# DeltaNet chunk matrices: decays from rows broadcast by DMA instead of a matmul and a transpose

## The chip, the cores and the metric

The kernel runs on one core of one Trainium2 chip. The metric is the device time of one execution in microseconds; the median of several executions is compared. The engines are called PE (TensorE, matmuls), DVE (VectorE), ACT (ScalarE), POOL (GpSimd) and SP (SyncE, which issues most DMAs). Each runs its own queue in order, and waits for the others through semaphores.

## What is computed

One step of a hybrid decoder layer for 256 prompt tokens and for 8 sequences of 4 new tokens (32 sample tokens), in float32. The reference, cut to the part around the change:

```python
h = RMSNorm(x);  q, k, v, z, beta, alpha, ... = split(h @ w_in)       # one projection, 15888 columns
g  = -exp(a_log) * softplus(alpha + dt_bias)                          # decay of a token and head
gc = cumsum(g) within a chunk
diff  = gc[..., :, None] - gc[..., None, :]
decay = where(incl, exp(where(incl, diff, 0)), 0)                     # incl: lower triangle with diagonal
lower = where(strict, (k*beta @ k.T) * decay, 0)                      # strict: without diagonal
tinv  = triangular_solve(eye + lower, eye)
u, w  = tinv @ (v*beta), tinv @ (k*beta*exp(gc))
a_intra = where(incl, (q @ k.T) * decay, 0)
# then a scan over the chunks with the state s0, a gated norm, two more branches
# (dilated attention, pooling), their merge through w_out, and a SwiGLU (w_gu, w_down)
```

There are 8 heads with keys and values of 128. `beta` is sigmoid of its projection, and k and q are scaled to length one.

## The kernel before

All 288 tokens (256 prompt, 32 sample) are the moving side of every dense matmul, 128 x 288; the weights stream in as the stationary side. A weight tile of 512 KB is loaded by SP (`raw`, L169), rounded by ACT to its high part (`wh`, L180), and DVE takes the rest (`wl`, L184). A dense product in float32 is made of three matmuls: wh with the high part of the activations (L256), wh with their low part (L257), wl with the high part (L258). There are some 14,000 of them; they are called dense matmuls here, and are counted to name a place in the program. There are five buffers of `raw` and three each of `wh` and `wl`.

The rest of the layer (the mixer) is written as Python generators, the convolution, `gdn(hg)` for the two head groups hg = 0 and 1 of four heads each, the attention, the pooling. After every weight tile, `step()` advances each of the running generators by its rate (a `yield n` counts n times). So the mixer's instructions come to stand between dense matmuls; a scheduler that plans with a timeline of its own then fixes the order in which each engine's queue stands. At run time nothing is reordered.

`beta_alpha` makes `beta` and the decays `g` for both groups and sums them with triangular ones matrices, `U` (row t, column i, one where t <= i), `V` (t > i) and block versions `Ub` and `Vb` for the sample tokens (blocks of four). It keeps exponentials of the sums (`egc`, `esf`, `egl`) and `g` itself (`gl`). `cp` tiles live through the mixer; `U(...)` takes one of NU slots of 128 x 288.

`gdn(hg)` handles nine matrices of 128 x 128 (x = 0 to 7: four heads times two stretches of 128 prompt tokens; x = 8: the sample tokens of the four heads). Before the change lies the normalisation: `ss` holds 1/|k| and 1/|q| (`rk`, `rq`), `s` = beta/|k|, and `nbe`, `kdc`, `qsc` are scales made from them (L710 to L713). Then, for each x, `gram` holds K K^T and K Q^T (L722); the decay matrix is a matmul of V with U scaled by the decays (`ug`, L720, L723), its exponential (ACT, L726) and a multiplication with U (POOL, L727); `s` is spread along the rows by a transpose of a broadcast column (L724); and DVE multiplies (L730, L732) to `la`, the masked and scaled matrices. `gram` tiles come from a ring of four PSUM buffers. From `la` POOL and DVE pick the diagonal 32 x 32 blocks (`lt`, `ltc`); these go to DRAM (`dlt`, L744) and come back as 32 small systems in 32 partitions (`lb`, L746), which DVE solves in 31 steps of two operations (`tm` L759, `X` L761). Between them, `gdn_sample` does the sample tokens, reading the state by SP (`st`, L891; `st2`, L953): the products `kss` of state and keys (L896), `ys` (L907), `zs` (L911) and `ws` (L915). The copy `ys` (DVE, L912) between `zs` and `ws` stands in DVE's queue among the steps of the solve. The kept matrices x = 0 to 7 go on to the merge of blocks (L775 on), and to the chunk scan.

Of the kernel before, what the change touches and what calls it, by code (L numbers as in the profile page):

```python
# [9 lines left out]
F32 = mybir.dt.float32  # L10
F32R = mybir.dt.float32r
AF = mybir.ActivationFunctionType
OP = mybir.AluOpType
# [6 lines left out]
NU = 98  # L20
# [68 lines left out]
class Layer:  # L89
# [335 lines left out]
    def beta_alpha(self):  # L425
        nc, a, c = self.nc, self.a, self.c
# [4 lines left out]
        p = self.ps("ba")  # L431
        for k in range(4):
            for j in range(4):
                d = j * 4 + k
                nc.tensor.matmul(p[32 * j:32 * j + 32, :NT], lhsT=w[:, d * 16:d * 16 + 32], rhs=self.xT[d],
                                 start=k == 0, stop=k == 3, tile_position=(0, 32 * j))
# [4 lines left out]
        for ch in range(2):  # L441
            nc.tensor.matmul(pt[:, ch * 16:ch * 16 + 16], lhsT=bat[:, ch * 128:(ch + 1) * 128], rhs=c["gsel"],
                             start=True, stop=True)
# [5 lines left out]
        beta = self.cp.tile([128, 2, 9], F32, name="beta")  # L449
# [45 lines left out]
        self.beta, self.gl, self.egc, self.esf, self.egl = beta, g, egc, esf, egl  # L495
# [6 lines left out]
        for hg in range(2):  # L502
            t = ts[hg]
            nc.tensor.matmul(pe[:, hg * 32:hg * 32 + 32], lhsT=c["ones"], rhs=t, start=True, stop=True)
            t2 = self.cp.tile([128, 32], F32, name=f"eglx{hg}")
            nc.scalar.activation(t2, pe[:, hg * 32:hg * 32 + 32], AF.Exp)
            self.egls.append(t2)

# [171 lines left out]
    def gdn(self, hg):  # L680
# [3 lines left out]
        gcol = lambda x: self.gl[:, hg * 9 + x:hg * 9 + x + 1]  # L684
# [29 lines left out]
        yield  # L714
        LA = {}
        ltc = pp.tile([128, 8, 32], F32, name="ltc")
        for x in X9:
            um, vm = (c["Ub"], c["Vb"]) if x == 8 else (c["U"], c["V"])
            ug = self.U(name="ug")
            nc.scalar.activation(ug[:, :128], um, AF.Copy, scale=gcol(x))  # L720
            p = self.ps("gram")
            nc.tensor.matmul(p[:, 0:256], lhsT=kq(x)[:, 0:128], rhs=kq(x)[:, 0:256], start=True, stop=True)  # L722
            nc.tensor.matmul(p[:, 256:384], lhsT=vm, rhs=ug[:, :128], start=True, stop=True)  # L723
            nc.tensor.transpose(p[:, 384:512], s[:, x:x + 1].to_broadcast([128, 128]), c["ident"])  # L724
            dt = ug[:, 128:256]
            nc.scalar.activation(dt, p[:, 256:384], AF.Exp)  # L726
            nc.gpsimd.tensor_tensor(dt, dt, um, op=OP.mult)  # L727
            la = self.U(name="la")
            for q in range(2):
                nc.vector.scalar_tensor_tensor(la[:, q * 128:q * 128 + 128], p[:, q * 128:q * 128 + 128],  # L730
                                               rk[:, x:x + 1], dt, op0=OP.mult, op1=OP.mult)
            nc.vector.tensor_tensor(la[:, 0:128], la[:, 0:128], p[:, 384:512], op=OP.mult)  # L732
            self.free(ug)
# [844 lines left out]
```

## Time and profile before

| | before |
|---|---|
| time, median of 3 runs | 2033.3 us |
| lowest, highest | 2032.03, 2034.34 us |
| the profiled execution | 2031.39 us |
| its span (first to last instruction) | 2029.6 us |
| mean granted clock of PE | 0.997 |

The span is what the views of the trace cover; the execution is 1.8 us longer than it. A row of the views begins with the start (us from the span's start) and the busy time; where instructions are grouped, "x36" counts them and a busy time covers the group. A row's bracket names the idle time before it and what ended it. PEclk and the granted clock are shares of PE's full speed. "SPq" rows are the issuing of DMAs, not their transfer. Matmul rows overlap, since matmuls are pipelined.

### The profile page before, as it was taken

Reading aid. Unit: us, or ns where it says so; the run is one execution under the profiler, and the core shown is the slowest. Engines: PE = TensorE matmul, PEld = TensorE weight load, DVE = VectorE, ACT = ScalarE, POOL = GpSimd, SP = SyncE. Lnnn points to the kernel's source line nnn. Section 1 sums busy time; section 2 is a strip of 40 time slices with the busy share of each in tenths; the row PEclk is TensorE's granted clock in tenths of the full one; section 3 lists DMA queues with packets and bytes.
Section 4 is the critical chain, followed back from the end, with each engine's and each line's share of the span. In section 5 each row is a group of like instructions: output and inputs, shape, how many; then the busy total and the mean of one; then the engine's idle time right before and its main releaser. Section 6 shows DMA issues by size and latency. Waiting matters only on the chain. (4 is left out here: it accounts for less than half of the span.)

```text
span 2029.6 us, 38724 instructions
## 1 busy us (share of the span) xinstructions
PE 2002.6 (99%) x15220; PEld 1979.3 (98%) x15220; DVE 1328.9 (65%) x2855; ACT 896.1 (44%) x1423; POOL 173.0 (9%) x315
## 2 busy tenths in 40 slices
PE   8999999999999999999999999999999999999998
PEld 8999998999999999999999999999999999999998
DVE  7969657658888779998874475544555445554555
ACT  6664464354444344333344454343333333333344
POOL 2325402300000031100000000000000000000001
PEclk9999999999999999999999999999999999999999
DMA  8565646758875567876667656777777677777762
GB/s 272 154 187 167 186 133 184 216 173 278 259 220 170 179 192 218 251 257 210 208 232 232 211 183 218 225 220 226 223 225 222 219 228 220 225 221 228 215 207 91
DMA packets 231350, 425.34 MB, mean 210 GB/s; under 512 B 23344, under 2 KB 67328, under 8 KB 229504
## 3 DMA queue, kind: packets, MB, share of 16 engines
q1 hardware_dynamic: 229856, 420.84, 66.8%
q8 instruction: 119, 1.95, 0.4%
q0 software_dynamic: 1168, 1.45, 0.2%
q10 hardware_dynamic: 144, 0.59, 0.1%
q14 instruction: 63, 0.52, 0.1%
HBM read 410.44 MB, written 66.63 MB: 235 GB/s over the span
## 5 line engine op out<-in xcount | busy, mean ns | idle before, releaser
L184 DVE TENSOR_TENSOR wl<-raw,wh 128x1024 fp32r<-128x1024 f32 x585 | 719.5, 1231 | 515.4 <-ACT wh L180 509.9
L180 ACT CAST wh<-raw 128x1024 fp32r<-128x1024 f32 x585 | 612.7, 1050 | 917.7 <-PE m L257 813.8
L256 PE MATMUL m<-hh,wh 128*128 128x288 f32 x1792 | 533.2, 299 | 0.3 <-DVE xp L1254 0.2
L257 PE MATMUL m<-hl,wh 128*128 128x288 f32 x1792 | 530.4, 297 | 0.0
L258 PE MATMUL m<-hh,wl 128*128 128x288 f32 x1792 | 522.5, 298 | 1.4 <-DVE wl L184 1.4
L257 PE MATMUL m<-xgl,wh 128*128 128x288 f32 x1408 | 413.7, 295 | 0.2 <-DVE xgl L1397 0.2
L256 PE MATMUL m<-xgh,wh 128*128 128x288 f32 x1408 | 410.2, 296 | 3.3 <-ACT xgh L1393 2.6
L258 PE MATMUL m<-xgh,wl 128*128 128x288 f32 x1408 | 412.9, 295 | 0.1
L257 PEld LDWEIGHTS m<-hl,wh 128*128 128x128 f32 x1792 | 338.4, 189 | 1.9 <-issue 1.8
L256 PEld LDWEIGHTS m<-hh,wh 128*128 128x128 f32 x1792 | 337.7, 189 | 2.4 <-issue 1.4
L258 PEld LDWEIGHTS m<-hh,wl 128*128 128x128 f32 x1792 | 334.7, 189 | 4.9 <-issue 3.0
L256 PEld LDWEIGHTS m<-xgh,wh 128*128 128x128 f32 x1408 | 264.3, 189 | 4.1 <-ACT xgh L1393 3.0
L257 PEld LDWEIGHTS m<-xgl,wh 128*128 128x128 f32 x1408 | 265.2, 188 | 0.7 <-DVE xgl L1397 0.7
L258 PEld LDWEIGHTS m<-xgh,wl 128*128 128x128 f32 x1408 | 265.1, 189 | 0.3 <-DVE wl L184 0.3
L257 PE MATMUL m<-hidl,wh 128*128 128x288 f32 x704 | 207.2, 295 | 0.0
L256 PE MATMUL m<-hidh,wh 128*128 128x288 f32 x704 | 206.9, 294 | 0.0
L258 PE MATMUL m<-hidh,wl 128*128 128x288 f32 x704 | 206.4, 295 | 0.0
L256 PEld LDWEIGHTS m<-hidh,wh 128*128 128x128 f32 x704 | 132.3, 188 | 0.0
L257 PEld LDWEIGHTS m<-hidl,wh 128*128 128x128 f32 x704 | 132.2, 188 | 0.0
L258 PEld LDWEIGHTS m<-hidh,wl 128*128 128x128 f32 x704 | 132.0, 188 | 0.0
L1506 POOL TENSOR_TENSOR yo<-y,xr 128x288 f32<-128x288 f32 x7 | 5.3, 795 | 1090.0 <-DVE y L1497 1090.0
L257 PE MATMUL m<-mgl,wh 128*128 128x288 f32 x256 | 75.1, 295 | 0.0
(384 smaller groups left out, 2574.0 us busy)
## 6 DMA issues: line engine op xcount, KB each, us to landing
raw<-w_in SPq DMA_DIRECT2D x247, 512.0 KB
raw<-w_gu SPq DMA_DIRECT2D x176, 512.0 KB
raw<-w_down SPq DMA_DIRECT2D x88, 512.0 KB
win_sample<-cache_win SPq DMA_DIRECT2D x64, 512.0 KB
kr<-cache_win SPq DMA_DIRECT2D x112, 256.0 KB
raw<-w_out SPq DMA_DIRECT2D x32, 512.0 KB
win_sample<-cache_win SPq DMA_DIRECT2D x32, 508.0 KB
st<-state_gdn SPq DMA_DIRECT2D x64, 128.0 KB
```

Of the source, the lines that this page charges most:

```text
L180: i = nc.scalar.copy(wh, raw)
L184: self.last_wl = nc.vector.tensor_tensor(wl, raw, wh.bitcast(F32), op=OP.subtract)
L256: nc.tensor.matmul(out, lhsT=wh[:, c], rhs=xh, start=k == 0, stop=False)
L257: nc.tensor.matmul(out, lhsT=wh[:, c], rhs=xl, start=False, stop=False)
L258: nc.tensor.matmul(out, lhsT=wl[:, c], rhs=xh, start=False, stop=k == nk - 1)
L1506: (nc.vector if how == "v" else nc.gpsimd).tensor_tensor(out[:, d % 2], y, x, op=OP.add)
```

## The change

The cumulated decays are kept (`gc`, in place of `g`) and transposed once for both groups; the 18 rows of 128 values go to DRAM (`drw[:, 1]`, L515). Each group then transposes `s` (nine rows) and writes it beside them (`drw[:, 0]`, L727). For each x one DMA reads the row pair of 256 values into all 128 partitions (`rw`, L735): columns 0 to 127 hold `s` of token i, columns 128 to 255 the cumulated decay of token i. DVE subtracts the partition's own cumulated decay and clips at 0 (L742), ACT takes the exponential in place (L743), POOL multiplies with U or Ub (L744) and then the `s` half with the result (L745). One DVE operation of 128 x 256 (L762) gives `la`. The matmul with V, the transpose of the broadcast column and `ug` are gone. The code starts two rows ahead, `yield` before them counts 2, and there are 100 slots instead of 98.

```diff
@@ -17,7 +17,7 @@
 
 NT, NP, NS = 288, 256, 32
 D, DFF, N_IN = 2048, 5632, 15888
-NU = 98
+NU = 100
 TPRE = 5
 TS = 6
 TAIL = 'eeeqqqeeeqqqeeqe'
@@ -492,7 +492,10 @@
             if k < 2:
                 v = pc[:, 128 + k * 32:128 + k * 32 + 18].rearrange("p (g x) -> p g x", g=2)
                 nc.scalar.activation(dst[:, :, 8:9], v[:, :, 8:9], AF.Exp)
-        self.beta, self.gl, self.egc, self.esf, self.egl = beta, g, egc, esf, egl
+        self.gc = self.cp.tile([128, 2, 9], F32, name="gc")
+        nc.vector.tensor_copy(self.gc[:, :, 0:8], pc[:, 0:18].rearrange("p (g x) -> p g x", g=2)[:, :, 0:8])
+        nc.vector.tensor_copy(self.gc[:, :, 8:9], pc[:, 128:146].rearrange("p (g x) -> p g x", g=2)[:, :, 8:9])
+        self.beta, self.egc, self.esf, self.egl = beta, egc, esf, egl
         self.egls = []
         ts = [self.cp.tile([128, 32], F32, name=f"egls{hg}") for hg in range(2)]
         for hg in range(2):
@@ -505,6 +508,12 @@
             t2 = self.cp.tile([128, 32], F32, name=f"eglx{hg}")
             nc.scalar.activation(t2, pe[:, hg * 32:hg * 32 + 32], AF.Exp)
             self.egls.append(t2)
+        nc.tensor.transpose(pe[:18, 128:256], self.gc.rearrange("p g x -> p (g x)"), c["ident"])
+        gt = self.U(name="gcT")
+        nc.scalar.copy(gt[:18, :128], pe[:18, 128:256])
+        self.drw = self.dr.tile([18, 2, 128], F32, name="drw")
+        nc.sync.dma_start(self.drw[:, 1], gt[:18, :128])
+        self.free(gt)
 
 
     def mixer_plan(self):
@@ -681,7 +690,7 @@
         nc, c, G, pp = self.nc, self.c, self.G[hg], self.pap
         beta, egc, esf = self.beta[:, hg], self.egc[:, hg], self.esf[:, hg]
         egl = self.egl[:, hg]
-        gcol = lambda x: self.gl[:, hg * 9 + x:hg * 9 + x + 1]
+        gcol = lambda x: self.gc[:, hg, x:x + 1]
         kq = lambda x: G["kqs"] if x == 8 else G["kq"][x // 2][x % 2]
         ss = self.small(18, "ss").rearrange("p (q x) -> p q x", q=2)
         kn = [self.U(name="kn") for _ in range(4)] + [self.U(name="kns")]
@@ -711,26 +720,48 @@
         nc.vector.scalar_tensor_tensor(nbe, s, -1.0, egc, op0=OP.mult, op1=OP.mult)
         nc.vector.tensor_tensor(kdc, rk, esf, op=OP.mult)
         nc.vector.tensor_scalar(qsc, rq, SC, None, op0=OP.mult)
-        yield
+        p = self.ps("sT9")
+        nc.tensor.transpose(p[:9, 0:128], s, c["ident"])
+        t = self.U(name="sT9")
+        nc.scalar.copy(t[:9, :128], p[:9, 0:128])
+        nc.sync.dma_start(self.drw[hg * 9:hg * 9 + 9, 0], t[:9, :128])
+        self.free(t)
+        rows, todo = deque(), deque(X9)
+
+        def load_row():
+
+            x = todo.popleft()
+            rw = self.U(name="rw")
+            nc.sync.dma_start(rw[:, 0:256], self.drw[hg * 9 + x].rearrange("q t -> (q t)")[None, :].to_broadcast([128, 256]))
+            rows.append((x, rw))
+
+        def decays():
+
+            x, rw = rows.popleft()
+            dt = rw[:, 128:256]
+            nc.vector.tensor_scalar(dt, dt, gcol(x), 0.0, op0=OP.subtract, op1=OP.min)
+            nc.scalar.activation(dt, dt, AF.Exp)
+            nc.gpsimd.tensor_tensor(dt, dt, c["Ub"] if x == 8 else c["U"], op=OP.mult)
+            nc.gpsimd.tensor_tensor(rw[:, 0:128], rw[:, 0:128], dt, op=OP.mult)
+            return rw
+
+        load_row()
+        load_row()
+        yield 2
         LA = {}
+        nxt = decays()
         ltc = pp.tile([128, 8, 32], F32, name="ltc")
         for x in X9:
-            um, vm = (c["Ub"], c["Vb"]) if x == 8 else (c["U"], c["V"])
-            ug = self.U(name="ug")
-            nc.scalar.activation(ug[:, :128], um, AF.Copy, scale=gcol(x))
+            rw = nxt
+            if todo:
+                load_row()
+            nxt = decays() if rows else None
             p = self.ps("gram")
             nc.tensor.matmul(p[:, 0:256], lhsT=kq(x)[:, 0:128], rhs=kq(x)[:, 0:256], start=True, stop=True)
-            nc.tensor.matmul(p[:, 256:384], lhsT=vm, rhs=ug[:, :128], start=True, stop=True)
-            nc.tensor.transpose(p[:, 384:512], s[:, x:x + 1].to_broadcast([128, 128]), c["ident"])
-            dt = ug[:, 128:256]
-            nc.scalar.activation(dt, p[:, 256:384], AF.Exp)
-            nc.gpsimd.tensor_tensor(dt, dt, um, op=OP.mult)
             la = self.U(name="la")
-            for q in range(2):
-                nc.vector.scalar_tensor_tensor(la[:, q * 128:q * 128 + 128], p[:, q * 128:q * 128 + 128],
-                                               rk[:, x:x + 1], dt, op0=OP.mult, op1=OP.mult)
-            nc.vector.tensor_tensor(la[:, 0:128], la[:, 0:128], p[:, 384:512], op=OP.mult)
-            self.free(ug)
+            nc.vector.scalar_tensor_tensor(la[:, 0:256], p[:, 0:256], rk[:, x:x + 1], rw[:, 0:256],
+                                           op0=OP.mult, op1=OP.mult)
+            self.free(rw)
             LA[x] = la
             if x < 8:
                 t = self.U(name="lt4")

```

The order of the queues follows from the scheduler's plan. Three places, word for word. In SP's queue in the first group (`raw` are weight tiles, `st` the state's loads, `drw` the DRAM tile), before:

```order
L169 DMA raw_2156<-w_in 128x2x512 [waits DMAHW4_49,DVE_49]
L891 DMA st_213_1878<-state_gdn 128x2x128 [waits DMAHW5_49,Activation_49]
L891 DMA st_214_1888<-state_gdn 128x2x128 [waits DMAHW6_49,Activation_49]
L891 DMA st_219_1948<-state_gdn 128x2x128 [waits DMAHW7_49,PE_49]
L891 DMA st_215_1890<-state_gdn 128x2x128 [waits DMAHW0_49,Activation_49]
L891 DMA st_220_1958<-state_gdn 128x2x128 [waits DMAHW1_49,PE_49]
L891 DMA st_216_1900<-state_gdn 128x2x128 [waits DMAHW2_49,Activation_49]
L169 DMA raw_2218<-w_in 128x2x512 [waits DMAHW3_49,DVE_49]
L169 DMA raw_2268<-w_in 128x2x512 [waits DMAHW4_49,DVE_49]
L169 DMA raw_2312<-w_in 128x2x512 [waits DMAHW5_49,DVE_49]
```

and now:

```order
L169 DMA raw_2211<-w_in 128x2x512 [waits DMAHW4_49,DVE_49]
L727 DMA drw_1200<-sT9_171_1572 9x128 [waits DMAHW5_49,Activation_49]
L735 DMA rw_172_1575<-drw_1200 128x256 [waits DMAHW6_49,DMAHW5_49]
L735 DMA rw_173_1577<-drw_1200 128x256 [waits DMAHW7_49]
L735 DMA rw_174_1644<-drw_1200 128x256 [waits DMAHW0_49]
L735 DMA rw_177_1684<-drw_1200 128x256 [waits DMAHW1_49]
L735 DMA rw_181_1697<-drw_1200 128x256 [waits DMAHW2_49]
L735 DMA rw_185_1710<-drw_1200 128x256 [waits DMAHW3_49]
L735 DMA rw_189_1723<-drw_1200 128x256 [waits DMAHW4_49]
L735 DMA rw_193_1766<-drw_1200 128x256
L735 DMA rw_197_1779<-drw_1200 128x256 [waits DMAHW6_49]
L922 DMA st_226_1951<-state_gdn 128x2x128 [waits DMAHW7_49]
```

The write of `s` and the nine reads stand in one block, and most state loads now come behind it. In DVE's queue behind the scales of the first group, now:

```order
L184 TENSOR_TENSOR wl_1910<-raw_1907,wh_1909 128x1024 [waits DMAHW2_49,PE_49,Activation_49]
L184 TENSOR_TENSOR wl_1988<-raw_1985,wh_1987 128x1024 [waits DMAHW3_49,PE_49,Activation_49]
L742 TENSOR_SCALAR rw_172_1575<-rw_172_1575,gc_1105 128x128 [waits DMAHW6_49]
L742 TENSOR_SCALAR rw_173_1577<-rw_173_1577,gc_1105 128x128 [waits DMAHW7_49]
L742 TENSOR_SCALAR rw_174_1644<-rw_174_1644,gc_1105 128x128 [waits DMAHW0_49]
L742 TENSOR_SCALAR rw_177_1684<-rw_177_1684,gc_1105 128x128 [waits DMAHW1_49]
L742 TENSOR_SCALAR rw_181_1697<-rw_181_1697,gc_1105 128x128 [waits DMAHW2_49]
L184 TENSOR_TENSOR wl_2051<-raw_2048,wh_2050 128x1024 [waits DMAHW4_49,PE_49,Activation_49]
L742 TENSOR_SCALAR rw_185_1710<-rw_185_1710,gc_1105 128x128 [waits DMAHW3_49]
L742 TENSOR_SCALAR rw_189_1723<-rw_189_1723,gc_1105 128x128 [waits DMAHW4_49]
L742 TENSOR_SCALAR rw_193_1766<-rw_193_1766,gc_1105 128x128 [waits DMAHW5_49]
L742 TENSOR_SCALAR rw_197_1779<-rw_197_1779,gc_1105 128x128 [waits DMAHW6_49]
```

The first row waits for its weight tile as before; nine operations on the rows that the DMAs bring stand around the weight tile `wl_2051`, ahead of the first `la`, where before the queue had L730 and L732 of the first matrices. In PE's queue now, at the 791st dense matmul and at the 864th, with the dense matmuls between them left out but for one at either side:

```order
L258 MATMUL m_1905<-hh_82_773,wl_1739 128x288
L724 MATMUL sT9_170_1570<-cc_81,s_1562 9x128 [waits DVE_49]
L760 MATMUL gram_175_1650<-ev_21_157 128x256
L760 MATMUL gram_178_1690<-ev_13_149 128x256
L760 MATMUL gram_182_1703<-ev_14_150 128x256
L256 MATMUL m_1905<-hh_86_828,wh_1738 128x288
...
L258 MATMUL m_1906<-hh_109_1057,wl_1988 128x288
L760 MATMUL gram_190_1729<-ev_16_152 128x256 [waits DVE_49]
L256 MATMUL m_1903<-hh_113_1114,wh_2050 128x288 [waits Activation_49]
```

The transpose of `s` and three grams stand together; a fourth follows 17 dense matmuls later, and the fifth, which waits for DVE, 73 dense matmuls behind the first three. Before, four sets of gram, decay matmul and transpose stood ahead of the 791st dense matmul, and four more from the 815th to the 817th. In the second group the transpose stands at the 1943rd dense matmul and the fifth gram at the 2017th.

## The prediction

> **What bounds the kernel now.** The page comes first: the engines' busy shares, then the chain that ended last.
>
> ```profile
> span 2029.6 us, 38724 instructions
> ...
> PE 2002.6 (99%) x15220; PEld 1979.3 (98%) x15220; DVE 1328.9 (65%) x2855; ACT 896.1 (44%) x1423; POOL 173.0 (9%) x315
> ...
> PE 48%; ACT 1%; DVE 0%; issue 0%; DVEq 0%; ACTq 0%
> ```
>
> TensorE is busy for 99% of the span, and the chain is TensorE work. So a microsecond of matmuls taken out of its queue is a microsecond of the kernel, unless TensorE then waits for something that it found ready before. Whether it does is read where the change works. Both programs have the same TensorE order from the 3270th dense matmul on, which leaves the first 480 us or so; the first steps of the two head groups lie in these windows (columns: span of time, its length, busy time and instructions of PE, PEld, DVE, ACT, POOL, granted clock, DMA share, GB/s):
>
> ```profile
> 100.00:150.00 50.00, 49.86 (x475) 48.53 (x473) 31.87 (x89) 33.38 (x101) 13.50 (x24) 1.00 0.65 184
> 150.00:200.00 50.00, 47.63 (x324) 44.10 (x325) 48.41 (x127) 20.40 (x42) 25.55 (x40) 0.97 0.59 179
> ...
> 300.00:350.00 50.00, 46.85 (x446) 43.90 (x445) 36.38 (x110) 25.95 (x69) 14.19 (x25) 1.00 0.71 203
> ```
>
> TensorE is idle for 0.14, 2.37 and 3.15 us there, and from 150 us on VectorE is busy for 48.41 of 50 us. The list of TensorE's waits names what ended these gaps:
>
> ```profile
> PE gram L722 <- DVE la L732: 1.9, 1, 1.9
> PE ws L915 <- DVE ys L912: 1.8, 1, 1.8
> ...
> PE kss L896 <- DMA st<-state_gdn: 1.3, 1, 1.3
> ```
>
> The first and third belong to the second head group, the `ws` wait to the first. Such waits are what the saving has to pass.
>
> **What is removed and added on TensorE.** The timeline of TensorE while three matrices follow each other:
>
> ```profile
> 128.25 0.29 PE L256 MATMUL m<-hh,wh 128*128 128x288 f32 x1
> 128.38 0.30 PE L257 MATMUL m<-hl,wh 128*128 128x288 f32 x1
> ...
> 130.32 0.59 PE L722 MATMUL gram<-ev 128*128 128x256 f32 x2
> 130.75 0.38 PE L723 MATMUL gram<-ug,cc 128*128 128x128 f32 x2
> 130.97 0.27 PE L724 MATMUL gram<-cc,s 128*128 128x128 f32 x1
> 131.08 0.60 PE L722 MATMUL gram<-ev 128*128 128x256 f32 x2
> ```
>
> Matmuls are pipelined, so the cost is from start to start. A dense matmul takes 0.13 us (128.25 to 128.38), the gram 0.43 (130.32 to 130.75), the decay matmul L723 0.22 (130.75 to 130.97), the transpose L724 0.11 (130.97 to 131.08). The last two go: 0.33 us a matrix. Their count:
>
> ```profile
> L723 PE MATMUL gram<-ug,cc 128*128 128x128 f32 x36 | 6.9, 274 | 0.0
> L724 PE MATMUL gram<-cc,s 128*128 128x128 f32 x18 | 4.1, 273 | 0.0
> ```
>
> That is 18 matrices (L723 counts twice, as an fp32 matmul is two instructions): 18 x 0.33 = 5.9 us. Three transposes of the same kind come in (of the summed decays, and of the factors `s` of each group), 0.3 us. **TensorE's work falls by 5.6 us**: 2.75 in the first group (with the common transpose), 2.86 in the second.
>
> **The other engines.** VectorE's groups (busy us, mean ns of one, idle before):
>
> ```profile
> L184 DVE TENSOR_TENSOR wl<-raw,wh 128x1024 fp32r<-128x1024 f32 x585 | 719.5, 1231 | 515.4 <-ACT wh L180 509.9
> ...
> L730 DVE SCALAR_TENSOR_TENSOR la<-gram,ss,ug 128x128 f32<-128x128 f32 x36 | 10.3, 341 | 2.1 <-POOL ug L727 2.1
> L732 DVE TENSOR_TENSOR la<-la,gram 128x128 f32<-128x128 f32 x18 | 4.6, 277 | 0.0
> ```
>
> It loses two L730 and one L732 a matrix (0.34 + 0.34 + 0.28) and gains an L742 of L732's size and an L762 of twice L730's: the trace shows neither, but with L762 between one L730 and two, the pair takes 0.62 to 0.96; between 0.3 us less a matrix and nothing. I take nothing, the end at which elements count. ScalarE loses L720. GpSimd gets one multiplication more per matrix. It is 9% busy; what matters is its chain, below. These costs lie beside dense matmuls; none is charged.
>
> **The new chain in the first group.** The factors `s` and what ScalarE and SyncE do after them:
>
> ```profile
> 119.94 0.17 DVE L710 TENSOR_TENSOR s<-beta,ss 128x9 f32<-128x9 f32 x1
> 120.23 2.45 ACT L787 ACTIVATE kn<-kn,kdc 128x128 f32<-128x128 f32 x8 [0.34 <-DVE kdc L712]
> 122.86 1.05 ACT L180 CAST wh<-raw 128x1024 fp32r<-128x1024 f32 x1
> 125.17 0.29 PE L256 MATMUL m<-hh,wh 128*128 128x288 f32 x1
> ```
>
> The transpose of `s` stands at the 791st dense matmul, which starts at 125.17 now; by then four gram sets have run that now come later (4 x 0.76 = 3.0), so TensorE is there at 122.2. Its copy stands on ScalarE behind a cast (1.05) and the eight `kn` (2.45): 120.2 + 1.05 + 0.1 + 2.45 = 123.8. Then SyncE writes 9 x 128 values to DRAM and reads nine rows back, in one block, each row a DMA of 128 KB. Neither DMA is in the trace; the nearest are the write `dlt` and the read of it, `lb`, which go the same way:
>
> ```profile
> 140.24 0.42 SPq L744 DMA_DIRECT2D dlt<-ltc  x1
> 140.75 2.60 SPq L953 DMA_DIRECT2D st<-state_gdn  x3
> 144.54 0.34 SPq L746 DMA_DIRECT2D lb<-dlt  x1
> 144.99 3.45 SPq L953 DMA_DIRECT2D st<-state_gdn  x7
> ...
> 147.01 0.18 DVE L759 TENSOR_TENSOR tm<-lb,X 32x31 f32<-32x31 f32 x1 [6.85 <-DMA lb<-dlt]
> ```
>
> From `dlt` to the issue that waits for it pass 4.30 us, from `lb` to its first reader 2.47; issues follow each other by 3.45 / 7 = 0.49. So the write takes 2.47 to 4.30 and the first row another 2.47: it is there at 123.9 + 4.94 = 128.8 to 123.9 + 6.77 = 130.7; I take the middle, 129.7, as the write is small like `lb` but raw tiles are on the way. The ninth row comes 8 x 0.49 later, 133.7 (132.8 to 134.7). On VectorE the first `la` stands behind all nine L742, so it ends about 0.9 later, at 134.6.
>
> TensorE meanwhile does the transpose, four grams and 73 dense matmuls: 122.2 + 0.11 + 1.72 + 9.7 = 133.7. There the fifth gram needs the first gram's PSUM buffer back, that is the first `la`: **a wait of 0 to 1.9 us, taken as 0.9**. In the old program a gram was ready as soon as its `ug` was; this wait is new in the first group.
>
> **The solve behind it.** GpSimd's row gives the pace of its multiplications, and two rows the old end of the chain:
>
> ```profile
> 125.88 1.72 POOL L727 TENSOR_TENSOR ug<-ug,cc 128x128 f32<-128x128 f32 x4 [4.90 <-ACT ug L726]
> 130.16 3.67 POOL L727 TENSOR_TENSOR ug<-ug,cc 128x128 f32<-128x128 f32 x4
> ...
> 151.34 0.27 DVE L912 COPY ys<-zs 128x128 f32<-128x128 f32 x1
> ```
>
> At 0.43 each, 29 operations (18 on the rows, 8 `lt`, 3 `x1s`) from 130.3 end at 142.8; a reduce, like an L730, takes 0.34 more, so 143.2. By the rows above, `dlt` to the first `tm` of the solve took 147.01 - 140.24 = 6.8, plus 0.3 before its issue: the solve starts at 150.3 instead of 147.01. The copy `ys` stands 13 solve operations behind its start, in both programs, 151.34 - 147.01 = 4.3 later: 154.7, so `ws` can start at 155.0. TensorE would be there, without a wait, after 96 dense matmuls, five grams, the `kss` pass and two small ones from the fifth gram on:
>
> ```profile
> 135.75 3.70 PE L896 MATMUL kss<-st,kz 128*32 128x128 f32 x128
> ```
>
> 133.7 + 12.7 + 2.15 + 3.6 + 0.4 = 152.6. So **TensorE waits 2.4 us in all** on this way, however it is split between the fifth gram, `kss` (its state loads now stand behind the nine rows on SyncE) and `ws`. In the old program it waited here too, and paid for it twice:
>
> ```profile
> 149.57 0.29 PE L257 MATMUL m<-hl,wh 128*128 128x288 f32 x1
> 151.67 0.49 PE L915 MATMUL ws<-ys,x1s 128*128 128x128 f32 x2 [1.80 <-DVE ys L912]
> ...
> 152.00:155.50 3.50, 3.50 (x18) 3.50 (x17) 3.40 (x8) 0.00 (x0) 0.00 (x0) 0.52 0.72 238
> ```
>
> The gap is 151.67 - 149.57 - 0.13 = 2.0 us; after it the granted clock was 0.52 for 3.5 us, 1.7 us of work lost. The new waits are together longer than that gap, but split. I count half of the 1.7 as coming back (0.85). First group: 2.75 + 2.0 + 0.85 - 2.4 = **3.2 us gained**.
>
> The Trainium skill has a rule here: "TensorE: Matmul & The Clock Gate", section "HAM oscillation — how this bites in real kernels", says that idle gaps beyond some 3.4 us cost the clock. By that rule no wait forecast here halves it and the whole 1.7 would be gained, which makes the time 0.85 less. The trace does not agree with the length: the clock fell behind a gap of 2.0 us.
>
> **The second group.** There the order is the same (fifth gram 74 dense matmuls behind the transposes), and the old program waits already:
>
> ```profile
> 321.28 0.27 PE L724 MATMUL gram<-cc,s 128*128 128x128 f32 x1
> 323.43 0.67 PE L722 MATMUL gram<-ev 128*128 128x256 f32 x2 [1.88 <-DVE la L732]
> ...
> 328.87 0.29 PE L257 MATMUL m<-hl,wh 128*128 128x288 f32 x1
> 330.43 0.65 PE L896 MATMUL kss<-st,kz 128*32 128x128 f32 x16 [1.27 <-DMA st<-state_gdn]
> ```
>
> 2.0 us at the gram and 1.4 at `kss`, 3.4 in all. The same chain as in the first group would make 2.4 of new waits; as more loads are on the way here (0.71 against 0.65 in the windows) I take them as long as the old ones. That leaves the saved work, **2.8 us** (3.8 with waits of 2.4). Sum: 3.2 + 2.8 = 6.0 us. The profiled execution took 2031.39, 1.8 more than its span; 2031.4 - 6.0 = 2025.4. It lies 1.9 below the median of the three runs, 2033.3, so the forecast is **2027.3**.
>
> What is queued behind the new waits: on VectorE a weight tile's `wl` stands behind five L742, the next behind all nine and the first `la`. That one is first used 27 dense matmuls behind the fifth gram, 3.6 us later, and needs 1.2 us (an L184): covered by some 2 us. On ScalarE casts stand between the exponentials, with the same cover; on SyncE the raw tile behind the nine rows is first needed at `ws`, 20 us later.
>
> **The rivals.** Let L be by how much the rows, and with them `la` and the solve, come later than computed. Each microsecond costs one in each group, since nothing else ends the waits.
>
> *Given back.* The write takes its upper end and the rows queue behind raw tiles, or GpSimd takes for four of its 29 operations what its second row shows, 0.92 each, 2 us more. For it: SyncE's one queue, and VectorE 48.41 of 50 busy. Against: half of the DMA price that I took is already queueing. L of 2: 6.0 - 4.0 leaves 2.0, **2031.3**. The time is within 0.2% (4.1 us, about what a measurement of this kernel can tell from no change) from L = 1.0 up to about 3.8.
>
> *Slower: the rows by DMA replace TensorE's work as the limit.* One mechanism at one place, the fifth gram: nine reads of one short DRAM row by 128 partitions each may move far slower than `lb`. If write and rows each take 4.3 and the block of nine spreads by as much again, L is 4.5; a gap of over 4 us at the gram also halves the clock in both groups (0.85 that I had counted as gained, and 1.7 in the second). 2 x 4.5 + 2.55 = 11.5, less 6.0: 5.5 us slower, **2038.8**. It is slower by over 0.2% from L = 3.8 on. Against it: 128 KB state loads are issued 0.49 apart.
>
> *All waits go.* With the write and row at 2.47, and `la` there before the fifth gram, both groups lose their old waits and the clock stays: 2.75 + 2.0 + 1.7 and 2.86 + 3.4, 12.7, less 1.0 each at `kss`, which is behind the rows anyway: 10.7, **2022.6**. Against: the copy behind ScalarE's `kn`, and GpSimd's 12.5 us of chain.
>
> **How the numbers follow.** Forecast 0.45 (2025 to 2029.2), given back 0.30, slower 0.15, all waits gone 0.10. The range leaves out the far part of the last two: 2023.5 to 2037. Faster by over 0.2% (under 2029.2): 0.55; within: 0.30; slower (over 2037.4): 0.15.
>
> **What would show it.** The decay matmuls and the transposes of `s` gone from TensorE's groups, three small transposes in. In the first group a wait of about 1 us of a gram for `la`, the solve's first `tm` at about 150 us, `ws` at about 155, and whether the clock falls in the 4 us behind it; in the second a wait at the fifth gram under 2.5 us. In the DMA issues, the rows' time to landing: 2.5 us bears the sum out, 5 and more the rivals. A weight tile that TensorE waits for behind the L742 would make it wrong, and so would a halved clock at a place not named.

## The result

The change makes the kernel slower: 2055.43 us (median of 4 runs, 2052.41 to 2058.71) against 2032.66 (median of 4 of before), ratio 1.0111 with a 95% interval of 1.0096 to 1.0127. That is 22.8 us more, where 6.0 less was forecast; it lies far outside the range.

The head of the page and the chain of the changed kernel:

```profile
span 2050.6 us, 38644 instructions
...
PE 2010.6 (98%) x15169; PEld 1984.5 (97%) x15169; DVE 1331.6 (65%) x2839; ACT 892.6 (44%) x1408; POOL 187.7 (9%) x333
...
PE 47%; ACT 1%; DVE 1%; issue 0%; DVEq 0%; ACTq 0%
```

TensorE has 51 instructions fewer and is busy 8 us longer. A busy time that grows with less work means slower matmuls. The stretch in which the change acts, first of before, then of after (length, busy PE, PEld, DVE, ACT, POOL, granted clock, DMA share, GB/s):

```profile
100.00:550.00 450.00, 442.65 (x3525) 431.36 (x3524) 321.16 (x899) 224.54 (x502) 98.35 (x164) 1.00 0.66 197
```

```profile
100.00:550.00 450.00, 428.16 (x3311) 413.92 (x3310) 306.77 (x817) 209.58 (x469) 112.99 (x182) 0.97 0.64 190
```

TensorE is idle for 7.4 us before and 21.8 after: 14.5 us more. Its mean clock falls from 1.00 to 0.97, which is some 13 us of work not done (450 x 0.03, give or take 2 for the rounding). With the 5.6 us of matmuls that were saved, 14.5 + 13 - 5.6 is about 22, and the span grew by 21.0. So all of the loss is waits and the halved clock behind them. The waits, in TensorE's list of after:

```profile
PE gram L760 <- DVE la L762: 5.6, 2, 3.2
...
PE ws L946 <- DVE ys L943: 4.3, 2, 2.4
PE kss L927 <- DMA st<-state_gdn: 2.9, 2, 1.9
PE m L812 <- POOL dd L806: 2.5, 1, 2.5
PE su L977 <- DVE st L988: 2.4, 1, 2.4
```

The forecast had three of these places, the grams, `kss` and `ws`, with 2.4 us in the first group and 3.4 in the second. There are five. The two waits at a gram are those of the fifth gram of each group:

```profile
136.73 1.22 PE L760 MATMUL gram<-ev 128*128 128x256 f32 x2 [2.40 <-DVE la L762]
339.21 0.70 PE L760 MATMUL gram<-ev 128*128 128x256 f32 x2 [3.21 <-DVE la L762]
```

The first group waits 2.4 us there, 2.4 at `ws` and 2.5 at `dd`, 7.3 in all; the second 3.2 at the gram, 2.9 at `kss`, 1.9 at `ws` and 2.4 at `su`, 10.4 in all. Six times the clock is about halved (windows of after), where the kernel before has one such stretch between 100 and 550 us:

```profile
136.40:139.80 3.40, 3.07 (x11) 2.90 (x12) 3.31 (x6) 1.67 (x4) 3.40 (x7) 0.50 0.75 216
161.50:167.00 5.50, 5.50 (x23) 5.50 (x24) 5.13 (x15) 0.00 (x0) 5.20 (x5) 0.50 0.65 197
366.00:371.00 5.00, 4.91 (x20) 4.77 (x20) 4.73 (x15) 2.15 (x5) 2.90 (x4) 0.50 0.64 200
375.00:381.50 6.50, 6.46 (x24) 5.70 (x24) 6.50 (x23) 1.19 (x3) 0.00 (x0) 0.52 0.31 91
238.00:242.20 4.20, 4.20 (x20) 4.20 (x21) 0.00 (x0) 0.27 (x1) 4.20 (x13) 0.59 0.80 268
481.10:484.50 3.40, 2.81 (x12) 2.75 (x13) 0.34 (x1) 1.17 (x3) 0.00 (x0) 0.50 0.33 99
```

In the order shown they stand at the first group's fifth gram and behind its `ws`, behind `ws` and `su` of the second group, behind `dd`, and among short waits at `ot` and `knat`. Now the new chain in the first group, by the timelines of VectorE, ScalarE, SyncE and GpSimd:

```profile
121.18 0.17 DVE L719 TENSOR_TENSOR s<-beta,ss 128x9 f32<-128x9 f32 x1
124.62 0.24 ACT L726 COPY sT<-sT 9x128 f32<-9x128 f32 x1
124.89 0.30 SPq L727 DMA_DIRECT2D drw<-sT  x1
126.97 4.14 SPq L735 DMA_DIRECT2D rw<-drw  x9
130.46 0.29 DVE L742 TENSOR_SCALAR rw<-rw,gc 128x128 f32<-128x128 f32 x1 [2.85 <-DMA rw<-drw]
131.71 0.38 SPq L922 DMA_DIRECT2D st<-state_gdn  x1
132.19 1.36 POOL L744 TENSOR_TENSOR rw<-rw,cc 128x128 f32<-128x128 f32 x3 [10.06 <-ACT rw L743]
136.20 0.47 DVE L762 SCALAR_TENSOR_TENSOR la<-gram,ss,rw 128x256 f32<-128x256 f32 x1
139.63 1.44 POOL L745 TENSOR_TENSOR rw<-rw 128x128 f32<-128x128 f32 x1
147.69 0.40 POOL L768 TENSOR_TENSOR lt<-la,cc 128x128 f32<-128x128 f32 x1 [0.22 <-DVE la L762]
154.86 0.18 DVE L790 TENSOR_TENSOR tm<-lb,X 32x31 f32<-32x31 f32 x1 [5.84 <-DMA lb<-dlt]
```

From `s` to the first `la` pass 15.0 us (121.18 to 136.20). In the kernel before, `s` was at 119.94 and VectorE's first `la` at

```profile
126.37 1.13 DVE L730 SCALAR_TENSOR_TENSOR la<-gram,ss,ug 128x128 f32<-128x128 f32 x4 [1.20 <-POOL ug L727]
```

6.4 us later. The solve starts at 154.86, against 147.01 before and 150.3 in the forecast. GpSimd has no gap between 132.19 and 147.5: its 29 operations take 15.9 us, where the forecast had 12.5, and single ones of them take 1.4 (139.63). SyncE's rows show another thing: the state load behind the nine reads is issued at 131.71. TensorE waits for a state load in the second group only (2.9 us; 1.3 before); in the first it comes to `kss` at 144.71 and finds its data.

### The profile page after: what moved, and what is told of

It is laid out like the page before. It is cut to its first block, busy times and chain, and to the rows that moved or that the text cites. A ratio compares the mean times of both kernels' runs of the same rounds, so it can differ in the third digit from the quotient of the medians.

```text
span 2050.6 us, 38644 instructions
## 1 busy us (share of the span) xinstructions
PE 2010.6 (98%) x15169; PEld 1984.5 (97%) x15169; DVE 1331.6 (65%) x2839; ACT 892.6 (44%) x1408; POOL 187.7 (9%) x333
## 5 line engine op out<-in xcount | busy, mean ns | idle before, releaser
L256 PEld LDWEIGHTS m<-hh,wh 128*128 128x128 f32 x1792 | 341.9, 191 | 5.2 <-ACT ev L1011 1.4
```

The lines of the kernel that those rows point to most:

```text
L256: nc.tensor.matmul(out, lhsT=wh[:, c], rhs=xh, start=k == 0, stop=False)
```

## The experiments

All were timed beside the kernel before on the same chip. The medians come from several chips, so what counts is the ratio to the runs of before on the same chip. "Idle" is TensorE's idle time between 100 and 550 us in the profiled execution, by the window above.

| | time, us | ratio to before (95%) | idle, us |
|---|---|---|---|
| the change | 2055.43 | 1.0111 (1.0096 to 1.0127) | 21.8 |
| rows that need not wait for s | 2035.66 | 1.0011 (1.0001 to 1.0021) | 14.9 |
| before, less TensorE work | 2029.19 | 0.9978 (0.9968 to 0.9988) | 9.1 |
| before, with write and unused rows | 2045.21 | 1.0061 (1.0046 to 1.0076) | 13.8 |
| before, with the write alone | 2035.36 | 1.0011 (1.0001 to 1.0020) | |
| before, with unused rows alone | 2033.86 | 1.0008 (0.9999 to 1.0018) | |
| before, s through DRAM | 2035.69 | 1.0012 (1.0003 to 1.0022) | |
| before, solve later | 2036.89 | 1.0022 (1.0013 to 1.0031) | |
| the change in group 0 alone | 2043.68 | 1.0052 (1.0037 to 1.0067) | |
| the change in group 1 alone | 2041.03 | 1.0032 (1.0020 to 1.0043) | |
| the change, six yields | 2039.60 | 1.0036 (1.0024 to 1.0049) | 13.4 |
| the change, one yield | 2048.09 | 1.0062 (1.0043 to 1.0081) | 25.4 |
| s by transpose, one yield | 2029.43 | 0.9982 (0.9973 to 0.9991) | 7.5 |

### Is it the path from s, or the added work?

**Rows that need not wait for s.** The s half of `drw` is written in `beta_alpha`.

```diff
-        nc.scalar.copy(gt[:18, :128], pe[:18, 128:256])
+        nc.scalar.copy(gt[:18, 128:256], pe[:18, 128:256])
+        nc.scalar.activation(gt[:18, :128], pe[:18, 128:256], AF.Copy, scale=-1e-6)
...
-        nc.sync.dma_start(self.drw[hg * 9:hg * 9 + 9, 0], t[:9, :128])
```

> The change, but the rows' first half comes from a row written together with the summed decays (these, times a small constant) and not from s; the transpose of s, its copy and its write fall away, so the rows can be read before s is there. The values of the key factor are wrong. Theory 1, the late chain (s, transpose, copy behind the kn, write, read: the rows come some 5 us after TensorE's queue wants the first la, all later waits and halved clocks follow): most of the loss goes, 2024 to 2036 us. Rival, the work itself (18 reads of 128 KB, twice the GpSimd work, state loads behind the rows): it stays at 2046 to 2058.

2035.66 us: 20 of the 22.8 us are gone, with the same 18 reads, VectorE and GpSimd work. What hangs on s makes most of the loss: the path to the rows, and SyncE's queue that stands behind the write; this run takes away both. It is still not below before, though TensorE has 5.8 us less to do: idle 14.9 us. Its largest new wait stands far behind the grams, in the row of the waits

```profile
PE ot L888 <- ACT bv L884: 4.2, 1, 4.2
```

`ot` is the output of the first group's scan, near 290 us.

**The saving by itself.**

```diff
-            nc.tensor.matmul(p[:, 256:384], lhsT=vm, rhs=ug[:, :128], start=True, stop=True)
-            nc.tensor.transpose(p[:, 384:512], s[:, x:x + 1].to_broadcast([128, 128]), c["ident"])
...
-            nc.scalar.activation(dt, p[:, 256:384], AF.Exp)
+            nc.scalar.activation(dt, ug[:, :128], AF.Exp)
...
-            nc.vector.tensor_tensor(la[:, 0:128], la[:, 0:128], p[:, 384:512], op=OP.mult)
+            nc.vector.tensor_tensor(la[:, 0:128], la[:, 0:128], c["Vb"], op=OP.mult)
```

> The kernel before without the decay matmul and without the transpose of the broadcast s: the exponential is taken of the scaled mask, and a constant mask stands for the spread s (decays and key factors are wrong). TensorE has 5.9 us less to do and no new chain arises. If the saving is worth what the prediction gave it: 2025 to 2029 us. If waits take it back even without the rows: 2031 to 2034.

2029.19: 4.1 us of the 5.9 come out (the medians differ by 4.1, the ratio says 4.5); idle grows by 1.8. So the price of TensorE's work in the prediction fits, and between a quarter and a third is given back at waits even without a new chain.

**Write and reads with nobody waiting for them.** In the kernel before, ahead of the grams:

```diff
...
+        nc.tensor.transpose(p[:9, 0:128], s, c["ident"])
...
+        nc.scalar.copy(t[:9, :128], p[:9, 0:128])
...
+        nc.sync.dma_start(drw, t[:9, :128])
...
+        for x in X9:
...
+            nc.sync.dma_start(rw[:, 0:256].rearrange("p (q t) -> p q t", q=2), drw[x][None, None, :].to_broadcast([128, 2, 128]))
```

> The kernel before, and besides the transpose of s, its copy, its write and nine row reads of 128 KB for each group, whose data nobody uses. Late chain: no one waits for them, so 2032 to 2037 us (0.2 of transposes, some delay of the state loads behind them). Work itself (traffic, SyncE's queue): a good part of the 22.8 us shows, 2040 to 2056.

2045.21, some 12 us slower, in the range of the rival; the first theory alone expected 2032 to 2037. SyncE's timeline, TensorE's wait and its rows of `kss` in the first group:

```profile
124.35 0.37 SPq L722 DMA_DIRECT2D drw<-sT  x1
126.33 5.09 SPq L726 DMA_DIRECT2D rw<-drw  x9
132.01 6.21 SPq L902 DMA_DIRECT2D st<-state_gdn  x8
...
PE kss L907 <- DMA st<-state_gdn: 4.3, 3, 1.8
...
134.76 1.95 PE L907 MATMUL kss<-st,kz 128*32 128x128 f32 x64
137.93 3.37 PE L907 MATMUL kss<-st,kz 128*32 128x128 f32 x64 [1.22 <-DMA st<-state_gdn]
```

The `kss` pass of the first group takes from 134.76 to 141.30, 6.5 us, and took 3.7 before (the prediction shows its row). That isn't all of the 12 us: TensorE's list also has 2.9 at `dd`, 2.8 for one `wl` and 2.0 at `ot`, and the solve starts at 150.91, 3.9 later. Eight state loads stand behind the block, from 132.01 on. In the kernel before the state loads of this group were out by 119.6 and only weight tiles followed:

```profile
117.04 2.53 SPq L891 DMA_DIRECT2D st<-state_gdn  x4
119.92 13.57 SPq L169 DMA_DIRECT2D raw<-w_in  x4
```

Then each half alone: the write without reads, and the same reads from a weight matrix, for which nothing has to be ready.

```diff
+            nc.sync.dma_start(rw[:, 0:256], self.a["w_in"][0][x, 0:256][None, :].to_broadcast([128, 256]))
```

> The kernel before, and the transpose of s, its copy and its write to DRAM for each group, but no row reads. It splits the 12 us that write and unused rows cost together. If SyncE's queue standing still until s is copied and written is what counts: 2038 to 2046 us. If the nine reads of 128 KB are: within 0.2% of before, 2031 to 2037.

> The kernel before, and nine unused row broadcasts of 128 KB for each group, read from a weight matrix, so that nothing has to be ready for them. If the reads themselves (queue time of 0.5 us each and traffic) cost: 2038 to 2046 us. If only their wait for the write does: 2031 to 2037.

2035.36 and 2033.86. Nine reads that wait for nothing cost 1 to 2 us, hardly told from nothing, a write that waits for s costs 2, both together 12: it seems that the reads cost where the write holds them back, and with them the loads that the scheduler has put behind. The runs don't show this cleanly, since the scheduler issued the free reads of the first group 50 us earlier than the reads above, away from the last state loads:

```profile
68.61 2.71 SPq L719 DMA_DIRECT2D rw<-w_in  x6
```

**Issued by ScalarE.** `nc.scalar.dma_start` for write and reads.

> The change with the write of s and the row reads issued by ScalarE, which makes the copy, and not by SyncE: state and weight loads no longer stand behind them. The path from s to the rows keeps its length. If the path is what counts (late chain): 2046 to 2058 us. If the loads behind the block on SyncE are: 2032 to 2044.

2058.01 (ratio 1.0130, 1.0115 to 1.0145), no better; `PE gram` waits for `la` 8.6 us in all. TensorE has no wait for a state load (2.9 us in the change) and none for a weight tile; besides `gram` it waits 4.5 us at `dd`, 3.9 at `su`, 3.8 at `ws` and 3.6 at `ot`. So the loss is there without a wait for the loads behind the block. ScalarE stands still for the write in its own queue, and the casts behind it with it; what this adds was not measured.

**GpSimd's second product on VectorE.** `nc.vector.tensor_tensor` for L745.

> The change with the product of the s half and the decays made by VectorE and not by GpSimd. If GpSimd's 29 operations are what makes the solve late (the last lt at 148.1 us, 5.3 later than forecast): 2042 to 2050 us. If the arrival of the rows is: 2051 to 2058.

2059.08 (1.0127, 1.0110 to 1.0144), no better. It doesn't clear GpSimd: the last `lt` ends at 148.9 us, no earlier than in the change (148.1), but now GpSimd waits for `la` on VectorE, where in the change it had no gap. The work has moved from one engine of the chain to another.

### Is lateness enough?

In the kernel before, s goes through DRAM and nothing else changes; and, in another run, the blocks do.

```diff
+        nc.sync.dma_start(ds, s)
+        s = self.small(9, "s2")
+        nc.sync.dma_start(s, ds)
```

> The kernel before, with s written to DRAM and read back before it is spread and multiplied: s comes some 4 to 5 us later in each group (one write, one small read), and nothing else changes. If lateness of la alone makes the loss of the change: 2042 to 2055 us. If it takes the block of reads on SyncE with the state loads behind it as well: 2033 to 2041.

```diff
...
+        nc.sync.dma_start(dl2, dlt)
+        dlt = dl2
```

> The kernel before, with one more copy in DRAM between the blocks that are written out (dlt) and the systems that are read back (lb), in both groups: the solve starts some 3 to 5 us later, and nothing else is added. If lateness costs once in each group: 2037 to 2042 us. If it is met again at the later places of TensorE's fixed order (dd, su, ot) and halves the clock: 2043 to 2055. If the scheduler's order has room for it: 2031 to 2036.

The solves of these two start at

```profile
151.66 0.18 DVE L763 TENSOR_TENSOR tm<-lb,X 32x31 f32<-32x31 f32 x1 [6.20 <-DMA lb<-dlt]
```

```profile
149.98 0.18 DVE L762 TENSOR_TENSOR tm<-lb,X 32x31 f32<-32x31 f32 x1 [3.87 <-DMA lb<-dl]
```

that is 4.7 and 3.0 us later than in the kernel before, and the times are 2035.69 and 2036.89: 2.4 and 4.5 us by the ratios. What TensorE waits for at `ws` is the copy `ys`, in the same order of the runs:

```profile
155.65 0.27 DVE L916 COPY ys<-zs 128x128 f32<-128x128 f32 x1
```

```profile
151.36 0.27 DVE L915 COPY ys<-zs 128x128 f32<-128x128 f32 x1
```

It was at 151.34. So the later solve doesn't reach `ws`: the scheduler has put `ys` further ahead, and this run tests less than it should. With s through DRAM `ys` comes 4.3 later. There the first group costs nearly that: the 1000th dense matmul starts at 170.79, where it started at 167.15. At the 3270th, behind both groups, 2.7 us are left (543.26, before 540.60): the second group's solve is later too, but its old waits shrink, 1.9 us at the gram to 1.2 and 1.3 at `kss` to none. So lateness doesn't cost one for one in each group: old waits take part of it up. But `la` comes 9.8 us later in the change and only 2.9 later here (129.31), and what a lateness as large as the change's would cost alone, no run shows.

**Distance between the reads and the first use.** The change with `yield 6`, and with `yield`, for `yield 2`:

> The change with four more steps of the generator between the row reads and the first use of a row, so that grams and solve stand later between the dense matmuls. Late chain: the waits at the fifth gram fall from 3 us to under 1 in both groups, the solve is later and dd waits instead; 2036 to 2050 us. Work itself: no gain, 2050 to 2060.

> The change with one yield ahead of the grams in place of two, so that grams stand earlier between the dense matmuls, or as now. Late chain: the rows come no earlier, so TensorE waits longer at the grams: 2055 to 2064 us. If the second yield was what disturbed an order that fitted: 2040 to 2050.

2039.60 and 2048.09: both are faster than the change, the second against what the late chain gave, and with six yields one gram still waits 2.6 us. Six yields give back 16 us with the same path and the same block; with one, the second group's grams all stand in one place and wait there once, for long (TensorE, timeline):

```profile
335.97 4.93 PE L760 MATMUL gram<-ev 128*128 128x256 f32 x8 [9.99 <-DVE la L762]
```

and yet this is 7 us better than several waits. So how the order falls around the path decides much of its price.

**One group at a time.**

> The change in the first head group alone, the second as before (with the common transpose and write of the summed decays). Late chain, which arises in each group by itself: about half of the 22.8 us, 2039 to 2049. If one group carries nearly all of it: under 2036 or over 2050.

> The change in the second head group alone. In the trace of the change TensorE falls back most behind the second group's ws (16 us between the 2112th and the 2300th dense matmul). Late chain: more than half, 2042 to 2050. If the second group suffers only because the first one is late: under 2038.

10.7 and 8.1 us by the medians (10.6 and 6.5 by the ratios), 18.8 of 22.8: each group by itself makes a loss, the second less than half, against what was expected. Part of the first group's price is paid in the second, whose code is the old one there and which waits at a gram for 4.2 us, 1.9 before:

```profile
PE gram L945 <- DVE la L955: 4.2, 1, 4.2
```

**A shorter path.** The copy of the transposed s by VectorE.

> The change with the copy of the transposed s made by VectorE, which is idle then, and not by ScalarE behind the eight kn (2.5 us): write and rows come some 2 us earlier. Late chain: each group gains about as much, 2045 to 2051 us. If the order of the queues and not the path's length decides: 2052 to 2058.

2055.13 (1.0097, 1.0078 to 1.0117). It did not test what it should: VectorE's copy stands behind a `wl` in its queue, and the write itself took longer, 128.35 to the first read at 131.56:

```profile
128.35 0.34 SPq L727 DMA_DIRECT2D drw<-sT  x1
131.56 2.72 SPq L735 DMA_DIRECT2D rw<-drw  x6
```

against 124.89 to 126.97 in the change.

### A version without the path

**s by transpose.** Rows carry the decays alone, which need only `beta_alpha`; s is spread on TensorE as before.

```diff
-            nc.sync.dma_start(rw[:, 0:256], self.drw[hg * 9 + x].rearrange("q t -> (q t)")[None, :].to_broadcast([128, 256]))
+            nc.sync.dma_start(rw[:, 128:256], self.drw[hg * 9 + x, 1][None, :].to_broadcast([128, 128]))
...
-            nc.gpsimd.tensor_tensor(rw[:, 0:128], rw[:, 0:128], dt, op=OP.mult)
...
+            nc.tensor.transpose(p[:, 384:512], s[:, x:x + 1].to_broadcast([128, 128]), c["ident"])
...
+            nc.vector.tensor_tensor(la[:, 0:128], la[:, 0:128], p[:, 384:512], op=OP.mult)
```

> Decays from rows by DMA, read early (they need only the summed decays); s spread by the old transpose on TensorE and multiplied by VectorE, one GpSimd product a matrix as before. TensorE saves 18 x 0.22 = 4.0 us less one transpose. Late chain: faster than before, 2026 to 2031 us. Work itself: the same number of reads with half the bytes stays, so 2036 to 2048.

2036.27 (1.0024, 1.0015 to 1.0034), at the lower end of the rival's range. Then with one yield, and with the decays finished at the start of `gdn`:

> The second experiment (s by transpose, decays by row reads) with one yield ahead of the grams as in the kernel before, in place of two. If the order against the dense matmuls makes its 3 us over the expected time: 2028 to 2033. If the reads do: 2035 to 2038.

> Decays by row reads as in the second experiment, but read at the start of gdn and finished (clipped difference, exponential, mask) while the keys are normalised; s by the old transpose on TensorE, one yield as before. Nothing of the decays is then behind s. Late chain: 2026 to 2032 us, as TensorE saves 3.8. If what was left there (2036) is a new order of the queues and not the decays' path: 2032 to 2038.

The first is **2029.43, faster than both kernels** (0.9982, 0.9973 to 0.9991); the second 2034.78 (1.0011, 1.0002 to 1.0020), in the range that it gave to a new order of the queues. In the faster one the reads go out early and TensorE's clock stays whole:

```profile
115.81 5.10 SPq L729 DMA_DIRECT2D rw<-drw  x9
...
150.00:200.00 50.00, 47.23 (x328) 42.95 (x327) 48.71 (x131) 21.20 (x43) 22.68 (x37) 1.00 0.64 184
```

Its idle time is 7.5 us, as before (7.4), so the 3.8 us that TensorE saves (18 x 0.22, less one transpose) come out as 3.5. It also lacks the halved stretch behind `ws` of before (1.7 us), so not all of the 3.5 need be the saving. One yield fewer is worth 7 us here. The rows without s with one yield were to show the same:

> The rows that do not wait for s (first experiment, key factors wrong), with one yield as before. With the path gone and an order near that of before, TensorE's 5.6 us should come out: 2026 to 2031. If waits behind a new order keep taking them: 2033 to 2038.

2037.97 (1.0017, 1.0007 to 1.0027), a miss. `ot` waits there as with two yields.

## Why the prediction was wrong

**Right.** TensorE was the bound, and the price of the work removed fits: less work alone gave 4.1 us of 5.9 while idle grew by 1.8, s by transpose with one yield 3.5 of 3.8. The chain of s, copy, write, reads, `la` and solve was the one that counts, and the fifth gram, `kss` and `ws` are places where it is met. The write took 2.1 us (124.89 to 126.97), below the price taken. Whether the new work of the other engines was rightly left at nothing is not shown: the rows without s keep it all, and lose 2.4 us where they save 5.8 on TensorE.

**The size of the chain.** `s` came 1.2 us later than in the kernel before (121.18), the first row at 130.46 for 129.7, the first `la` began at 136.20, where it was to end at 134.6, and the last `lt` ended at 148.1, not 142.8: GpSimd started 1.9 us later than forecast (132.19 for 130.3), and its 29 operations took 0.55 us each, not 0.43, 3.4 more. The solve was 4.6 us late against the forecast, about the L of the rival that was to be slower, 4.5. That the numbers agree is luck: the rival's place came true, the fifth gram in both groups, its mechanism, rows that move slowly, did not, as the write took half its price and the first row came 0.8 late. Its L doesn't follow from its own terms either, write and row of 4.3 each and a block twice as long, which make 2.8 for the first row and 6.7 for the ninth. Its price, 2038.8, was 17 us short.

**The step that failed** is what the sum has for waits and clock. It let the waits grow by 0.4 us in the first group (2.4 for 2.0) and by nothing in the second, and gained 0.85 of clock. Measured between 100 and 550 us, idle time grew by 14.5, and the clock took 13 more. Under it lies the rule by which all cases were priced: "Each microsecond costs one in each group, since nothing else ends the waits." The runs deny a fixed price from both sides. With s through DRAM, 4.3 us later at `ws` of the first group, the kernel lost 2.4, since old waits took part of it up. In the change the same chain is met at three places of the first group and four of the second, and behind five of these seven waits it is paid again in halved clock. With six yields, the same path and the same block cost 7 us and not 23.

**The state loads.** The prediction named them ("its state loads now stand behind the nine rows on SyncE") and gave them no price. In the kernel before, write and reads without a reader cost 12 us. This can't be taken off the 22.8 as a share: there the loads are met at `kss` of the first group, where the change waits for none, and that kernel lacks the saving of 5.6. In the change the wait for state loads grows by 1.6 us (2.9 for 1.3), the waits for the chain's own data (`la`, `ys`, `dd`, `st`) by 9.6 (14.8 for 5.2). So the late chain is the greater part by the trace; how much of its lateness the held loads cause is not shown.

**The places.** The forecast ended at `ws`. Waits at `dd` and `su`, and the clock halved behind them, weren't looked for: `su` of the second group follows its `ws` by 10 us, `dd` of the first by 78, and the order of the queues, which could be read, has both as waits for VectorE and GpSimd. For one halved stretch of clock, of which half was to come back, there are six; those behind `dd` and `su` and the last one stand at places that the prediction didn't name, which it had given as a sign of being wrong. The part in which the two orders differ is also longer than it said: the 3270th dense matmul starts at 540.6 us in the kernel before, not near 480.

**The second group** was to wait no longer than before, 3.4 us. It waited 10.4, at the gram, `kss`, `ws` and `su`. Before and after, with the stretch cut at the 1856th dense matmul, ahead of its chain:

```profile
100.00:306.20 206.20, 202.53 (x1612) 197.21 (x1611) 146.55 (x353) 112.86 (x290) 64.76 (x107) 0.99 0.58 169
306.20:550.00 243.80, 240.12 (x1915) 234.15 (x1914) 174.61 (x546) 111.69 (x212) 33.59 (x57) 1.00 0.72 221
```

```profile
100.00:309.60 209.60, 200.98 (x1566) 195.28 (x1564) 142.21 (x328) 104.11 (x246) 77.23 (x116) 0.97 0.57 168
309.60:550.00 240.40, 227.19 (x1748) 218.65 (x1747) 164.56 (x489) 105.47 (x225) 35.76 (x66) 0.96 0.70 209
```

Idle time grows from 3.7 to 8.6 us in the first part and from 3.7 to 13.2 in the second, which also has the lower clock. One reason is when its chain starts: its `s` comes at 322.77, where it came at 309.62. In the kernel with the change in the first group alone it is late as well, at

```profile
321.38 0.17 DVE L933 TENSOR_TENSOR s<-beta,ss 128x9 f32<-128x9 f32 x1
```

and with the change in the second group alone it is not:

```profile
304.45 0.17 DVE L719 TENSOR_TENSOR s<-beta,ss 128x9 f32<-128x9 f32 x1
```

So the changed first group hands lateness on. Why the scheduler's order does so was not tried.

**What stays open**: how the loss splits between the lateness of `la` and the loads that the write holds back, as no run has the change's full lateness without the other; and why the order with six yields suits the same path so much better than with two. Each edit made the scheduler plan anew, and the spread between neighbouring plans (7 us between one and two yields, twice) is as large as many effects measured here, so a single run's few microseconds, and part of the 12 for the unused rows, may be the plan's.

## What to carry to other kernels

A DMA round trip in the middle of a dependent chain can have two prices, the latency, and what the issuing queue holds up while it waits: look for the loads that stand behind. On the bound engine a wait can be paid twice, once as idle time and once as halved clock. Data that is known early should make the trip early and alone; only what comes late should stay on the engines. A saving on the bound engine counts only if the chain that meets it next has that much slack, and this must be followed past the first wait.

## What was not expected of the hardware

The clock. Waits of 2.0 to 2.5 us (the first group's fifth gram, `ws` twice, `su`, `dd`) were followed by stretches at about half speed, shown above in windows of 3.4 to 6.5 us, as the gap of 2.0 us in the kernel before had been; behind the fastest version's waits between 100 and 550 us, none of them over 1.2 us, it stayed at 1.00. But length doesn't decide alone: the longest wait at a gram, 3.2 us in the second group, left it whole in its window of after,

```profile
300.00:350.00 50.00, 44.80 (x371) 43.36 (x373) 31.51 (x69) 32.73 (x93) 16.64 (x33) 1.00 0.63 184
```

The rule that the prediction weighed, of the Trainium skill, "TensorE: Matmul & The Clock Gate", section "HAM oscillation — how this bites in real kernels", by which gaps beyond some 3.4 us cost the clock, does not agree with these traces: 2.0 us were enough in some places, and 3.2 not in another.

The reads. Nine reads that spread 1 KB of DRAM over 128 partitions were no dearer to issue than the state loads: 4.14 / 9 = 0.46 us each.
